# A two-layer diffusion trunk on one core: modulation weights in bursts, a narrow projection folded into a wide one, the convolution norm in more steps

## The chip, the cores and the metric

The kernel is one program on one core of a Trainium2 chip. The metric is the device time of that program in microseconds (us). All matrix work runs on TensorE (PE). VectorE is DVE, ScalarE is ACT, GpSimd is POOL; nearly all transfers are issued by SyncE (SP), whose queue is served in order. Each engine runs its own instructions strictly in the order of its queue, so an instruction that waits holds up all that stand behind it.

## The reference, cut to what matters

There are two token streams of 256 tokens, `x` and the context, with width 1024, and two layers. A layer modulates the normalized input by vectors computed from `c`, projects it, runs three branches (attention, gated linear attention or GLA, and a convolution module), merges them under gates, and ends with a feed-forward part.

```python
mod = (silu_c @ w_ada[l] + b_ada[l])[:, None, :]
sh1, sc1, g1, sh2, sc2, g2 = jnp.split(mod, 6, axis=-1)
proj = h @ p['w_in']
k, v, kg, vg, glr = _split(pm, MEM_SPLITS)        # glr: 32 columns, the low-rank gate input
k = _rmsnorm(_heads(k, N_KV_HEADS), p['k_norm'])
z = jnp.einsum('blnr,nrk->nblk', glr.reshape(B, L, 2, GLA_RANK), w_a2) + b_a[:, None, None, :]
o_gla = _rmsnorm(o_gla, p['gla_norm']).transpose(0, 2, 1, 3).reshape(B, L, GLA_V)
y = a * jax.nn.sigmoid(g)                          # then a depthwise convolution, 31 taps
y = jax.nn.silu(_layernorm(y, p['conv_ln_g'], p['conv_ln_b']))
return (g_att * y_att + g_gla * y_gla + g_conv * y_conv) @ p['w_out']
```

## The kernel before

Every large product is made of three matmuls in fp32r (`mm3`: high by high, high by low, low by high), because weights and activations are split into a high and a low part. A weight block of 128 x 1024 is loaded by SP into a `raw` buffer (5 of them), ACT copies it into `whi` (3 buffers), DVE subtracts into `wlo` (2 buffers); this is `wload`, lines 98 and 99. All large matmuls carry line 137. `fm` makes one feature-major product, 24 matmuls from one block. `tm` makes token-major products. Results lie in PSUM buffers of tag `mm` (4), `tr` (2) or `sd` (2).

Small work is written as Python generators (`attend`, `gla_head`, `conv_fin`, `ada_head`, `ada_gen`); `step` advances the first two in the list after each weight block, so their instructions fall between the large matmuls. Instructions are then put on the engines' queues by a planner with priorities, so the order of the queues is not that of the source.

`ada_head` computes the first two of a layer's modulation vectors: for each of four column groups j, four weight blocks of 512 KB (`ada`), eight fp32 matmuls at line 277 of 32 rows by 512 columns, each pair followed by a `yield`. The eight lie in four column groups of the array, `32 * (k % 4)`. In layer 0 it runs at the very start, with the loading and normalizing of the inputs (`run`, lines 815 to 834), and group j+1 is computed while the key and value projection (`kv`, with `start` called for each j) uses group j. In layer 1 it runs under the feed-forward part of layer 0. `ada_gen` does the rest of the vectors with four matmuls between yields (line 301).

`layer_consts` loads the taps, norms and rotation tables of a layer (`cols`, `qk`, `cs`). `gla_in` makes the inputs of a GLA head; `gla_prep` needs `glrT`, which is a whole `fm` product of its own from `wglr`, whose 128 columns are the 32 gate columns repeated. `gla_head` ends with a norm of each 128 x 256 output (`on`): ACT squares it with a sum (line 640), POOL makes the reciprocal root (93, 94), ACT copies it scaled (643), PE transposes it (649). `conv_fin` is the norm of the convolution: a matmul of ones over the sums (line 694) gives the means, DVE subtracts them from PSUM (702), ACT squares, POOL adds, a second product (714) gives the variance, DVE makes diagonal matrices (721), a third (725) spreads the reciprocal root, DVE multiplies from PSUM (731), ACT takes tanh and identity (737), and the result is split into `cvh` and `cvl` for the branch that multiplies by `w_conv_o`.

Of the kernel before, what the change touches and what calls it, by code (L numbers as in the profile page):

```python
# [52 lines left out]
class Trunk:  # L53
    BUFS = dict(hl=32, y=8, qt=8, kv=2, g=6, raw=5, whi=3, wlo=2, t4=4, tA=2, tB=4, pt=2, S=3, h1=6, sm=16, sa=16, sg=16, st=8,
                mc=4, cacc=1, jk=2, near=2)
# [198 lines left out]
    def ada_head(self, l, res):  # L254
# [8 lines left out]
        for j in range(4):  # L263
            ps = self.PS("sd")
            for i in range(4):
                if l == 0 and j % 2:
                    raw = [self.T("qt", [128, 512], name="ada") for _ in range(2)]
                    for kk in range(2):
                        nc.sync.dma_start(out=raw[kk], in_=I["w_ada0"][l, j, i][:, kk * 512:(kk + 1) * 512])
                else:  # L270
# [1 line left out]
                    nc.sync.dma_start(out=raw, in_=I["w_ada0"][l, j, i])
                    raw = [raw[:, :512], raw[:, 512:]]
                for kk in range(2):
                    k = 2 * i + kk
                    g = k % 4
                    nc.tensor.matmul(ps[32 * g:32 * g + 32, :], self.sc[:, k, :], raw[kk],  # L277
                                     start=(k < 4), stop=(k >= 4))
                yield
# [220 lines left out]
    def gla_head(self, h, kq, vg, og, last, me):  # L500
# [92 lines left out]
        for s in order:  # L593
# [35 lines left out]
            for c in range(2):  # L629
# [13 lines left out]
                nc.scalar.activation(out=on, in_=ps[:, :256], func=AF.Copy, scale=rs)  # L643
# [44 lines left out]
    def conv_fin(self, ys, ntok, hl):  # L688
# [5 lines left out]
        nc.tensor.matmul(pm[:, :ntok], self.onecol.to_broadcast([128, 128]), self.csum[:, :ntok], start=True, stop=True)
# [567 lines left out]
```

## Time and profile before

| | us |
|---|---|
| three runs | 1918.33, 1924.79, 1923.61 |
| median of them | 1923.61 |
| the profiled execution | 1923.12 |
| span of its instructions | 1921.1 |
| PE busy in the span | 1837.5 |
| DVE, ACT, POOL busy | 1300.9, 866.6, 167.5 |

The profiled execution lies 0.5 us under the median. Its time is 2.0 us more than the span. An idle time in brackets behind a row names what ended it. In rows of PE an fp32 matmul leaves two records, so "x4" on line 277 is two matmuls and "x8" on line 301 is four.

### The profile page before, as it was taken

The page shows a single profiled execution, that of the slowest core. Times are in us where ns is not written, and L with a number is a line of the kernel's source. Part 1 is how long each engine was busy: PE and PEld are TensorE (multiplying, and loading weights), DVE is VectorE, ACT ScalarE, POOL GpSimd, SP SyncE. Part 2 cuts the span into 40 slices and gives each one's busy share as a digit, 9 for nine tenths or more (in the row PEclk, how much of TensorE's full clock was granted, in tenths as well). Part 3 has the DMA queues.
Part 4 walks back from the last instruction along what each step waited for, and adds up shares of the span by engine and source line. Part 5 has one row for each costly group of instructions (what it writes and reads, how often), then busy time and mean ns, then how long its engine had stood idle before and what let it go on. Part 6 is the DMA issues. An engine that isn't in the chain of part 4 may idle for free.

```text
span 1921.1 us, 29251 instructions
## 1 busy us (share of the span) xinstructions
PE 1837.5 (96%) x11300; PEld 1498.2 (78%) x11300; DVE 1300.9 (68%) x2280; ACT 866.6 (45%) x1482; POOL 167.5 (9%) x235
## 2 busy tenths in 40 slices
PE   6999999999999999989999999989999999979998
PEld 2677788677777878867776888877888889969996
DVE  3597999987653445774333457689999777675656
ACT  2445434435733343453222334555455476445442
POOL 1111000012011001100000000031000200110000
PEclk8999999999999999989999999999999999989999
DMA  6421122632374334565466357643233435765663
GB/s 229 163 78 45 56 77 90 215 116 76 104 254 161 100 124 142 190 211 177 161 215 229 121 198 225 220 126 110 86 100 123 149 121 167 235 212 161 191 208 122
DMA packets 90892, 292.30 MB, mean 152 GB/s; under 512 B 10353, under 2 KB 12145, under 8 KB 90753
## 3 DMA queue, kind: packets, MB, share of 16 engines
q1 hardware_dynamic: 90752, 290.43, 46.8%
q8 instruction: 89, 1.46, 0.3%
q14 instruction: 51, 0.41, 0.1%
HBM read 277.77 MB, written 12.62 MB: 151 GB/s over the span
## 4 chain that ended last, share of the span: by engine, by line
PE 79%; DVE 10%; ACT 4%; issue 2%; POOL 2%; DMA 2%; SPq 0%; DVEq 0%; POOLq 0%; ACTq 0%
PE mm L137 66%; DVE acc L674 4%; DVE wlo L99 3%; PE sd L449 2%; PE sd L423 2%; PE sd L277 2%; PE mm L301 2%; PE sd L557 1%; PE sd L610 1%; ACT whi L98 1%; DMA ada<-in_w_ada 1%; PE sd L637 1%; PE tr L444 1%; POOL sg L94 1%; PE tr L344 1%
## 5 line engine op out<-in xcount | busy, mean ns | idle before, releaser
L99 DVE TENSOR_TENSOR wlo<-raw,whi 128x1024 fp32r<-128x1024 f32 x378 | 466.7, 1236 | 317.9 <-PE mm L137 230.9
L137 PE MATMUL mm<-hi,whi 128*128 128x512 f32 (+1 forms) x1920 | 657.5, 343 | 1.1 <-ACT whi L98 0.5
L137 PE MATMUL mm<-hi,wlo 128*128 128x512 f32 (+1 forms) x1920 | 650.5, 339 | 2.5 <-DVE wlo L99 2.3
L137 PE MATMUL mm<-lo,whi 128*128 128x512 f32 (+1 forms) x1920 | 651.4, 340 | 0.8 <-DVE lo L354 0.7
L98 ACT ACTIVATE whi<-raw 128x1024 fp32r<-128x1024 f32 x378 | 400.7, 1061 | 537.3 <-PE mm L137 416.8
L137 PEld LDWEIGHTS mm<-hi,whi 128*128 128x128 f32 x1920 | 364.5, 190 | 64.6 <-issue 12.7
L137 PEld LDWEIGHTS mm<-lo,whi 128*128 128x128 f32 x1920 | 365.2, 190 | 43.3 <-DVE lo L354 3.2
L137 PEld LDWEIGHTS mm<-hi,wlo 128*128 128x128 f32 x1920 | 364.5, 190 | 43.1 <-DVE wlo L99 4.8
L674 DVE SCALAR_TENSOR_TENSOR acc<-y,cols,acc 128x512 f32<-128x512 f32 (+1 forms) x464 | 288.5, 622 | 9.8 <-issue 0.2
L137 PE MATMUL mm<-wlo,hi 128*128 128x512 f32 (+1 forms) x676 | 238.6, 353 | 7.5 <-DVE wlo L99 7.5
L137 PE MATMUL mm<-whi,hi 128*128 128x512 f32 (+1 forms) x676 | 239.6, 356 | 0.6 <-ACT hi L352 0.6
L137 PE MATMUL mm<-whi,lo 128*128 128x512 f32 (+1 forms) x676 | 236.8, 351 | 0.0
L137 PEld LDWEIGHTS mm<-wlo,hi 128*128 128x128 f32 x676 | 127.6, 189 | 32.6 <-DVE wlo L99 9.9
L137 PEld LDWEIGHTS mm<-whi,hi 128*128 128x128 f32 x676 | 127.5, 189 | 22.1 <-issue 2.4
L137 PEld LDWEIGHTS mm<-whi,lo 128*128 128x128 f32 x676 | 127.5, 189 | 20.5 <-issue 2.5
L91 POOL TENSOR_SCALAR sm<-sm 128x1 f32<-128x1 f32 (+1 forms) x38 | 15.9, 418 | 756.9 <-DVE sm L332 664.6
L1036 POOL TENSOR_TENSOR mgp<-mgp,mgold 128x512 f32<-128x512 f32 x24 | 32.3, 1346 | 266.2 <-DVE mgp L1034 230.7
L277 PE MATMUL sd<-ada,sc 128*32 128x512 f32 x128 | 41.4, 703 | 11.8 <-DVE x L827 9.4
L449 PEld LDWEIGHTS sd<-pt,v 128*128 128x128 f32 x320 | 39.9, 191 | 16.0 <-ACT pt L446 12.1
L581 DVE TENSOR_TENSOR X<-X,sums 128x256 f32<-128x256 f32 (+1 forms) x112 | 47.6, 426 | 4.6 <-PE sd L557 3.3
L682 POOL TENSOR_TENSOR csum<-csum,y 128x512 f32<-128x512 f32 (+1 forms) x14 | 18.4, 1313 | 360.9 <-DVE y L674 360.9
L449 PE MATMUL sd<-pt,v 128*128 128x128 f32 x320 | 47.2, 286 | 2.6 <-ACT pt L446 1.1
(227 smaller groups left out, 2033.9 us busy)
## 6 DMA issues: line engine op xcount, KB each, us to landing
raw<-in_wfm SPq DMA_DIRECT2D x112, 512.0 KB
raw<-in_wff SPq DMA_DIRECT2D x94, 512.0 KB
raw<-in_wdown SPq DMA_DIRECT2D x66, 512.0 KB
raw<-in_w_ada SPq DMA_DIRECT2D x64, 512.0 KB
raw<-in_wbr SPq DMA_DIRECT2D x48, 512.0 KB
ada<-in_w_ada SPq DMA_DIRECT2D x24, 512.0 KB
raw<-in_wout SPq DMA_DIRECT2D x24, 512.0 KB
raw<-in_wq SPq DMA_DIRECT2D x16, 512.0 KB
```

The costliest lines, as they stand in the source:

```text
L94: nc.gpsimd.tensor_tensor(out=out, in0=t[:, :n], in1=self.mhalf.to_broadcast([128, n]), op=ALU.pow)
L98: nc.scalar.activation(out=hi, in_=src, func=AF.Copy)
L99: (eng or nc.vector).tensor_tensor(out=lo, in0=src, in1=hi.bitcast(F32), op=ALU.subtract)
L137: i = self.nc.tensor.matmul(*a, **k)
L277: nc.tensor.matmul(ps[32 * g:32 * g + 32, :], self.sc[:, k, :], raw[kk], start=(k < 4), stop=(k >= 4))
L301: nc.tensor.matmul(ps[32 * gg:32 * gg + 32, :], self.sc[:, k, :], raw[:, g * 512:(g + 1) * 512], start=(k == 0), stop=(k == KC - 1))
L344: nc.tensor.transpose(tr[:, kk, t * 128:(t + 1) * 128], xn[t][(k2 + kk) // 4][:, (k2 + kk) % 4 * 128:((k2 + kk) % 4 + 1) * 128], self.ident)
L423: nc.tensor.matmul(ps[:, :nk], qT[:, hh, :], self.kT[:, n, ko:512], start=True, stop=True)
L449: nc.tensor.matmul(po, self.v[:, ko // 128 + c, n * 128:(n + 1) * 128], pt[:, c, :], start=(c == 0), stop=(c == nkc - 1))
L581: nc.vector.tensor_tensor(out=a, in0=a, in1=t, op=ALU.mult)
L674: nc.vector.scalar_tensor_tensor(out=out, in0=win(y, sel, t), scalar=tap(t), in1=acc, op0=ALU.mult, op1=ALU.add)
L1036: nc.gpsimd.tensor_tensor(out=p, in0=p, in1=old, op=ALU.add)
```

## The change

- `ada_head`: in layer 0 all four blocks of a group are loaded and then all eight matmuls follow, the last block's first; in layer 1 two blocks at a time, four matmuls.
- `run` and `start`: all four input tiles are loaded ahead of the first modulation weights; they are normalized on ACT instead of DVE; `layer_consts(0)` comes after the third column group.
- `low_rank`: the 32 gate columns are appended to the value weights of GLA head 0 (`wvg0`, blocks of 128 x 1152, matmuls of 288 columns instead of 256); four copies on ACT repeat them, four transposes make `glrT`. The product from `wglr` is gone.
- `k_proc`: the scaling of the keys goes from DVE to POOL.
- `gla_head`: the output is copied out of PSUM unscaled and POOL scales it.
- `conv_fin`: three empty steps ahead of it, one ahead of each of the later products; means and reciprocal roots are copied by ACT into an SBUF buffer `cm`, from which DVE reads.

```diff
-                mc=4, cacc=1, jk=2, near=2)
+                mc=4, cacc=1, jk=2, near=2, cm=1)
-            raw = self.T("raw", [128, 1024])
+            raw = self.T("raw", [128, 1152])
...
-            for i in range(4):
...
-                for kk in range(2):
-                    k = 2 * i + kk
+            for n0 in (0,) if l == 0 else (0, 1):
+                parts = []
+                for i in range(4) if l == 0 else range(2 * n0, 2 * n0 + 2):
...
+                        parts += [(2 * i, raw[:, :512]), (2 * i + 1, raw[:, 512:])]
+                for n, (k, raw) in enumerate(parts[::-1]):
                     g = k % 4
-                    nc.tensor.matmul(ps[32 * g:32 * g + 32, :], self.sc[:, k, :], raw[kk],
-                                     start=(k < 4), stop=(k >= 4))
-                yield
+                    nc.tensor.matmul(ps[32 * g:32 * g + 32, :], self.sc[:, k, :], raw,
+                                     start=(n0 == 0 and n < 4), stop=(l > 0 and n0 == 1 or n >= 4))
+                if l:
+                    yield
...
-        nc.vector.tensor_tensor(out=kn, in0=kn, in1=rk.unsqueeze(2).to_broadcast([128, 2, 128]), op=ALU.mult)
+        nc.gpsimd.tensor_tensor(out=kn, in0=kn, in1=rk.unsqueeze(2).to_broadcast([128, 2, 128]), op=ALU.mult)
...
                 nc.scalar.activation(out=on, in_=ps[:, :256], func=AF.Square, accum_out=ss)
+                nc.scalar.activation(out=on, in_=ps[:, :256], func=AF.Copy)
                 rs = self.T("sg", [128, 1])
                 self.rstd(rs, ss, 1.0 / 256, EPS, 1, "sg")
-                nc.scalar.activation(out=on, in_=ps[:, :256], func=AF.Copy, scale=rs)
+                nc.gpsimd.tensor_tensor(out=on, in0=on, in1=rs.to_broadcast([128, 256]), op=ALU.mult)
...
+        for _ in range(3):
+            yield
         pm = self.PS("sd")
         nc.tensor.matmul(pm[:, :ntok], self.onecol.to_broadcast([128, 128]), self.csum[:, :ntok], start=True, stop=True)
+        cm = self.T("cm", [128, 512])
+        nc.scalar.activation(out=cm[:, :ntok], in_=pm[:, :ntok], func=AF.Copy)
...
+        yield
+        pv = self.PS("sd")
...
+        yield
         pr = self.PS("sd")
...
+        cm = self.T("cm", [128, 512])
+        nc.scalar.activation(out=cm[:, :ntok], in_=pr[:, :ntok], func=AF.Copy)
...
-        self.ada0 = self.ada_head(0, mod)
         for t in range(4):
-            if t == 2:
-                for _ in range(5):
-                    next(self.ada0)
...
-                nc.vector.tensor_scalar(out=x[n], in0=x[n], scalar1=mv[:, 0:1], scalar2=rs, op0=ALU.subtract,
-                                        op1=ALU.mult)
+                nc.scalar.activation(out=x[n], in_=x[n], func=AF.Identity, scale=rs, bias=nb)
             xn[t] = x
+        self.ada0 = self.ada_head(0, mod)
+        next(self.ada0)
         self.l = 0
-        self.layer_consts(0)
...
-            for _ in range(5):
-                next(self.ada0, None)
+            next(self.ada0, None)
+            if j == 2:
+                self.layer_consts(0)
...
-        pg = self.PS("mm")
-        self.fm(I["wglr"][l], pg, h)
...
+        def low_rank(g):
+
+            tr = self.PS("tr", (128, 4, 128))
+            for t in range(4):
+                nc.tensor.transpose(tr[:, t, :], g[:, t, :], self.ident)
...
+            n = 256 if hd else 288
+            ws = [self.wload(I["wvg"][l, hd, j] if hd else I["wvg0"][l, j], 4 * n, shift=112 if hd else 0) for j in range(2)]
```

The planner gives other queues. The first place is PE at the start, while column group 1 of layer 0's modulation (`ada`, into an `sd` buffer) is computed among the first matmuls of the key and value projection (`mm`, with `whi` and `wlo` its weights, `hi` and `lo` the modulated input). Before:

```order
L277 MATMUL sd_267<-ada_268,sc 32x512
L277 MATMUL sd_267<-ada_269,sc 32x512
L137 MATMUL mm_237<-whi_302,hi_202 128x512
L137 MATMUL mm_238<-whi_302,hi_202 128x512
L137 MATMUL mm_239<-whi_302,hi_202 128x512
L137 MATMUL mm_240<-whi_302,hi_202 128x512
L277 MATMUL sd_267<-ada_274,sc 32x512
L137 MATMUL mm_237<-wlo_303,hi_202 128x512
L137 MATMUL mm_237<-whi_302,lo_203 128x512
L137 MATMUL mm_237<-whi_302,hi_204 128x512
L277 MATMUL sd_267<-ada_275,sc 32x512
```

Now:

```order
L137 MATMUL mm_233<-whi_296,hi_196 128x512
L280 MATMUL sd_261<-ada_276,sc 32x512
L280 MATMUL sd_261<-ada_274,sc 32x512
L280 MATMUL sd_261<-ada_272,sc 32x512
L280 MATMUL sd_261<-ada_270,sc 32x512
L280 MATMUL sd_261<-ada_268,sc 32x512
L280 MATMUL sd_261<-ada_266,sc 32x512
L280 MATMUL sd_261<-ada_264,sc 32x512
L280 MATMUL sd_261<-ada_262,sc 32x512
L137 MATMUL mm_231<-whi_296,hi_198 128x512
L137 MATMUL mm_231<-wlo_297,hi_198 128x512
L137 MATMUL mm_231<-whi_296,lo_199 128x512
```

The eight matmuls that stood singly or in pairs among the projection's matmuls now stand in one run, and the first of them reads the block that is loaded last.

The second place is SP's queue at the same time. Before, behind the input tiles:

```order
L227 DMA cols_175<-in_cols 128x286
L234 DMA qk_180<-in_qknorm 128x256
L236 DMA cs_182<-in_cossin 128x512
L107 DMA raw_300<-in_wkv 128x1024
L269 DMA ada_268<-in_w_ada 128x512
L269 DMA ada_269<-in_w_ada 128x512
L269 DMA ada_274<-in_w_ada 128x512
L269 DMA ada_275<-in_w_ada 128x512
L269 DMA ada_280<-in_w_ada 128x512
L269 DMA ada_281<-in_w_ada 128x512
L269 DMA ada_286<-in_w_ada 128x512
L269 DMA ada_287<-in_w_ada 128x512
```

Now, behind the input tiles and the first column group:

```order
L276 DMA ada_165<-in_w_ada 128x1024
L107 DMA raw_294<-in_wkv 128x1024
L272 DMA ada_262<-in_w_ada 128x512
L272 DMA ada_264<-in_w_ada 128x512
L272 DMA ada_266<-in_w_ada 128x512
L272 DMA ada_268<-in_w_ada 128x512
L272 DMA ada_270<-in_w_ada 128x512
L272 DMA ada_272<-in_w_ada 128x512
L272 DMA ada_274<-in_w_ada 128x512
L272 DMA ada_276<-in_w_ada 128x512
L107 DMA raw_375<-in_wkv 128x1024
```

The three loads of `layer_consts(0)` (`cols`, `qk`, `cs`) are gone from this place; the first weight block and the second column group follow the first group at once.

The third place is ACT in layer 0, where GLA head 3's values are copied out of PSUM (`vg` from `mm`, ahead of the convolution's branch product). Before:

```order
L990 ACTIVATE kq_4623<-mm_4711 128x256
L98 ACTIVATE cvh_4822<-y_2560 128x512
L513 ACTIVATE X_4892<-kq_3785 128x2x256
L497 ACT_TABLE_LOAD
L497 ACTIVATE sums_4671<-sums_4671 128x1020
L497 ACTIVATE sums_4670<-sums_4670 128x1020
L98 ACTIVATE whi_5024<-raw_5022 128x1024
L1003 ACTIVATE vg_4624<-mm_4765 128x256
L1003 ACTIVATE vg_4624<-mm_4791 128x256
L1003 ACTIVATE vg_4625<-mm_4826 128x256
L1003 ACTIVATE vg_4625<-mm_4852 128x256
L539 ACTIVATE kk_4970<-X_4878 128x256
```

Now:

```order
L98 ACTIVATE cvh_4703<-y_774 128x512
L750 ACTIVATE y_1689<-y_1689,cols_464 128x2x256
L750 ACTIVATE th_4833<-y_2004,cols_464 128x512
L98 ACTIVATE cvh_4776<-y_1689 128x512
L98 ACTIVATE whi_5023<-raw_5021 128x1024
L750 ACTIVATE y_2004<-y_2004,cols_464 128x2x256
L750 ACTIVATE th_4842<-y_2271,cols_464 128x512
L750 ACTIVATE y_2271<-y_2271,cols_464 128x2x256
L98 ACTIVATE cvh_4837<-y_2004 128x512
L1024 ACTIVATE vg_4578<-mm_4719 128x256
L1024 ACTIVATE vg_4578<-mm_4745 128x256
L1024 ACTIVATE vg_4579<-mm_4780 128x256
```

Before, one of the norm's steps (`cvh`) stood within a dozen rows ahead of the copies; now eight of them (`th`, `y`, `cvh`) do, with a weight block among them.

More of the change, by code (lines that the diff above doesn't have):

```diff
@@ L116, in wload_hl @@
         with self.tc.high_priority(offset=self.ahead):
-            raw = self.T("raw", [128, 1024])
-            nc.sync.dma_start(out=raw, in_=src)
+            raw = self.T("raw", [128, 1152])
+            nc.sync.dma_start(out=raw[:, :1024], in_=src)
             his, los = [], []
@@ L295, in ada_gen @@
             for hf in range(2):
-                raw = self.T("raw", [128, 1024])
+                raw = self.T("raw", [128, 1152])
                 c0 = (r - 1) * 2048 + hf * 1024
-                nc.sync.dma_start(out=raw, in_=I["w_ada"][l, k * 128:(k + 1) * 128, c0:c0 + 1024])
+                nc.sync.dma_start(out=raw[:, :1024], in_=I["w_ada"][l, k * 128:(k + 1) * 128, c0:c0 + 1024])
                 for g in range(2):
@@ L699, in conv_fin @@
             yv = win(ys[g], slice(0, 2), 15)
-            mean = pm.rearrange("p (s t) -> p s t", t=256) if cpg == 1 else \
-                pm[:, :256].unsqueeze(1).to_broadcast([128, 2, 256])
+            mean = cm.rearrange("p (s t) -> p s t", t=256) if cpg == 1 else \
+                cm[:, :256].unsqueeze(1).to_broadcast([128, 2, 256])
             nc.vector.tensor_tensor(out=yv, in0=yv, in1=mean, op=ALU.subtract)
@@ L728, in conv_fin @@
             yv = win(ys[g], slice(0, 2), 15)
[L729 to L730 removed]
+            r = cm.rearrange("p (s t) -> p s t", t=256) if cpg == 1 else \
+                cm[:, :256].unsqueeze(1).to_broadcast([128, 2, 256])
             nc.vector.tensor_tensor(out=yv, in0=yv, in1=r, op=ALU.mult)
@@ L991, in gla_in @@
             step()
-            ws = [self.wload(I["wvg"][l, hd, j], shift=112) for j in range(2)]
+            n = 256 if hd else 288
+            ws = [self.wload(I["wvg"][l, hd, j] if hd else I["wvg0"][l, j], 4 * n, shift=112 if hd else 0) for j in range(2)]
+            if not hd:
+                low = self.T("tB", [128, 4, 128], name="low")
             for t in range(4):
-                ps = self.PS("mm", (128, 256))
+                ps = self.PS("mm", (128, n))
                 for k in range(KC):
                     hi, lo = ws[k // 4]
-                    s = slice(k % 4 * 256, (k % 4 + 1) * 256)
+                    s = slice(k % 4 * n, (k % 4 + 1) * n)
                     xh, xl = stat(t, k)
@@ L1002, in gla_in @@
                 with self.evac():
-                    nc.scalar.activation(out=vg[t // 2][:, t % 2, :], in_=ps, func=AF.Copy)
+                    nc.scalar.activation(out=vg[t // 2][:, t % 2, :], in_=ps[:, :256], func=AF.Copy)
+                    if not hd:
+                        nc.scalar.activation(
+                            out=low[:, t, :].rearrange("p (d r i) -> p d r i", d=2, r=4),
+                            in_=ps[:, 256:288].rearrange("p (d i) -> p d i", d=2).unsqueeze(2).to_broadcast(
+                                [128, 2, 4, 16]), func=AF.Copy)
                 if t % 2:
                     step()
+            if not hd:
+                low_rank(low)
             me = []
@@ L1227, in pack @@
     w2 = w2.reshape(L, 4, 128, 128)
-    glr = np.concatenate([2048 + 16 * d + np.arange(16) for d in (0, 0, 0, 0, 1, 1, 1, 1)])
+    vg0 = np.concatenate([w_in[:, :, 1024:1280], w_in[:, :, 2048:2080]], axis=2).reshape(L, 2, 4, 128, 288)
+    vg0 = vg0.transpose(0, 1, 3, 2, 4).reshape(L, 2, 128, 1152)
     cc = np.concatenate([np.broadcast_to(a.reshape(8, 128).T[:, :, None], (128, 8, 16)) for a in (c, c_ctx)], axis=2)
```

34 lines of the change are left out of this document (17 added, 17 removed).

## The prediction

> **What bounds the kernel now.** I read the page's busy times and the shares of the chain first, then what PE waited for, then the windows of the start.
>
> ```profile
> PE 1837.5 (96%) x11300; PEld 1498.2 (78%) x11300; DVE 1300.9 (68%) x2280; ACT 866.6 (45%) x1482; POOL 167.5 (9%) x235
> PE 79%; DVE 10%; ACT 4%; issue 2%; POOL 2%; DMA 2%; SPq 0%; DVEq 0%; POOLq 0%; ACTq 0%
> PE sd L277 <- DVE x L827: 9.4, 1, 9.4
> PE tr L649 <- ACT on L643: 6.5, 12, 1.2
> PE sd L694 <- POOL csum L682: 4.6, 2, 2.9
> PE sd L637 <- ACT on L643: 3.6, 4, 1.6
> PE sd L714 <- POOL csum L712: 1.3, 1, 1.3
> ```
>
> PE is busy 1837.5 of 1921.1 us and holds 79% of the chain, so a gain has to come from matrix work taken off PE, or from the start. The waits at the places that the change touches sum to 16 us beside the 9.4 us at the very start. The start, by windows, once for all engines (columns: window, PE, PEld, DVE, ACT, POOL, granted clock, DMA share, GB/s) and once for the modulation matmuls of line 277 alone (PE, PEld, clock, DMA):
>
> ```profile
> 0.00:9.30 9.30, 0.00 (x0) 0.00 (x0) 4.38 (x14) 1.70 (x2) 2.07 (x16) 1.00 0.75 241
> 9.30:25.60 16.30, 10.19 (x36) 2.98 (x36) 9.26 (x22) 3.64 (x7) 5.85 (x10) 0.79 1.04 407
> 25.60:40.90 15.30, 15.09 (x54) 7.09 (x52) 3.73 (x6) 2.71 (x6) 0.00 (x0) 0.89 0.15 48
> 25.60:40.90 15.30, 6.02 (x14) 0.74 (x12) 0.89 0.15 48
> 40.90:53.20 12.30, 4.25 (x19) 0.62 (x22) 1.00 0.79 273
> 53.20:66.50 13.30, 5.21 (x16) 0.66 (x16) 1.00 0.49 190
> 19.59 23.18 SPq L272 DMA_DIRECT2D ada<-in_w_ada  x4
> ```
>
> Up to 25.6 us the transfers are the limit (407 GB/s). From there PE is full, but only partly with the projection: of 40.9 us between 25.6 and 66.5, line 277 takes 6.02 + 4.25 + 5.21 = 15.5. The DMA share of 0.15 in the second stretch is SP standing for 23.18 us in the third group's loads, since `t4` buffers are taken.
>
> **Modulation in bursts.** The price of one insertion stands in layer 0's feed-forward part, where 24 matmuls alternate with one pair, and later with one group of four:
>
> ```profile
> 882.93 0.50 PE L137 MATMUL mm<-hi,whi 128*128 128x512 f32 x1
> 888.27 0.39 PE L137 MATMUL mm<-hi,wlo 128*128 128x512 f32 x1
> 888.59 1.05 PE L277 MATMUL sd<-ada,sc 128*32 128x512 f32 x4
> 889.57 0.50 PE L137 MATMUL mm<-hi,whi 128*128 128x512 f32 x1
> 946.42 0.39 PE L137 MATMUL mm<-hi,wlo 128*128 128x512 f32 x1
> 946.74 1.06 PE L301 MATMUL mm<-raw,sc 128*32 128x512 f32 x8
> 947.73 0.50 PE L137 MATMUL mm<-hi,whi 128*128 128x512 f32 x1
> 692.39 115.95 PE mm L137 x511
> ```
>
> A matmul of 512 columns takes 115.95 / 511 = 0.227 us, so 24 take 5.45; the period 882.93 to 889.57 is 6.64, so a pair costs 1.19. Four in four column groups cost the same: from the last matmul ahead of them to the first behind, 946.42 to 947.73 is 1.31, and 888.27 to 889.57 for the pair is 1.30. So the price goes by insertion, not by matmul.
>
> In layer 1's vectors PE's queue has 16 insertions before and 10 now; the six that go all lie behind the point where the feed-forward part runs without waits: 6 x 1.19 = 7.1 us. Ends: 3, if the held loads cost some of it back, and 9. I take -7.
>
> In layer 0 three groups fall among the projection, 15 insertions before, 3 runs of eight now. Eight are two rounds of four, 2 x 0.98 plus the change of form, some 2.1 us; three cost 6.3 instead of 15.5, a gain of 9.2 if the runs are warm. The first is not: the clock granted in these stretches is 0.79 and 0.89. On the other side, the first projection matmul starts at 25.6 now. The bytes ahead of it shrink by `cols`, `qk`, `cs` and the second group. Inputs and first group are 4.3 MB: 241 GB/s x 9.3 us are 2.2, the other 2.1 at 407 GB/s take 5.2, so they are in at 14.5 to 16 (the inputs' rows are half as long as the weights'). Eight matmuls at half the rate of the 0.98 per round take to 20, the copy, the small transposes and the modulation another 4 (an estimate). That is 24, a gain of 1.6, and about as much is lost again where the second run is cold too. I take -9 for the start. Ends: -3, if transfers keep setting the pace, and -13.
>
> `layer_consts(0)` comes later: `qk` now stands on SP behind the second block of the queries' weights. POOL's tables and keys wait for it, and so do PE's key transposes, which stand 84 matmuls x 0.227 = 19 us behind the projection in the queue. POOL needs some ten steps of 0.73 (row below) before the first of them, 8 us. So nothing, unless the load comes 10 us late; ends 0 and +5. The keys' scaling on POOL has the same cover. The inputs' normalization on ACT lies under the loading.
>
> **The low-rank product.** Per layer 24 matmuls of 512 columns go, 5.45 us. 96 matmuls grow by 32 columns. Nearest rows for 256 columns, and for transposes:
>
> ```profile
> 316.33 0.28 PE L137 MATMUL mm<-wlo,hi 128*128 128x256 f32 x1
> 316.45 0.28 PE L137 MATMUL mm<-whi,lo 128*128 128x256 f32 x1
> 65.41 1.03 PE L344 MATMUL tr<-ident,x 128*128 128x128 f32 x8
> ```
>
> 0.12 us per 256 columns is 0.015 per 32, 96 of them 1.4 us; four transposes of 1.03 / 8 = 0.13 and two changes of form are 0.8. So 5.45 - 2.2 = 3.2, twice 6.5 us less on PE. DVE and ACT lose one `wload` per layer and gain four small copies. New is a wait: `glrT` used to be ready long before its use; now 18 matmuls (4.1 us) cover ACT's copy and DVE's step, which stands behind two taps of 0.75. I charge +1 in all. Sum -5.5; ends -2 (wider matmuls at a worse rate) and -7.
>
> **Conv norm and GLA outputs.** The first product stands 38 matmuls later in layer 0 and 48 of half width in layer 1, over 5 us, against waits of 1.7 and 2.9: -4.6. The wait of 1.3 may stay, since POOL's chain of squares is the same; in layer 1 only 11 matmuls (1.3 us) now cover variance, root and diagonal, so +0.6. Together -4; ends -5.9 and 0.
>
> ```profile
> L643 ACT ACTIVATE on<-sd,sg 128x256 f32<-128x256 f32 x24 | 11.4, 473 | 19.9 <-POOL sg L94 19.9
> L387 POOL TENSOR_TENSOR kr<-kr,kn 128x256 f32<-128x256 f32 x4 | 2.9, 730 | 0.0
> ```
>
> The unscaled copy frees PSUM without POOL, so the 3.6 us at line 637 go. The chain to the transposes grows by 0.73 (POOL) less 0.47 (ACT), 0.3 with the queue 0.4; at some 8 of 24 places nothing covers it: +3.2. I take 0; ends -4 and +5.
>
> **A crowd that the queues show.** In layer 0 the second half of the conv norm now falls into the stretch in which GLA head 3's inputs are made. Between the third product of the norm and the copies of `vg`, ACT's queue holds 10 steps `th` and `y`, 4 `cvh`, 3 `whi`, 6 steps of `ea`, 2 of `sums`, 4 `kq`, 2 table loads and two small ones. Prices:
>
> ```profile
> 479.24 1.51 ACT L737 ACTIVATE y<-y,cols 128x512 f32<-128x512 f32 x2
> 498.41 1.27 ACT L481 ACTIVATE ea<-sd,cols 128x512 f32<-128x512 f32 x2
> 500.73 1.28 ACT L488 ACT_TABLE_LOAD   x1
> 503.09 1.05 ACT L98 ACTIVATE whi<-raw 128x1024 fp32r<-128x1024 f32 x1
> 504.04 0.63 ACT L990 ACTIVATE kq<-mm 128x256 f32<-128x256 f32 x2
> 504.56 0.63 ACT L98 ACTIVATE cvh<-y 128x512 fp32r<-128x512 f32 x1
> 507.83 2.00 ACT L497 ACTIVATE sums<-sums 128x1020 f32<-128x1020 f32 x2 [0.82 <-DVE sums L495]
> 516.40 1.21 ACT L1003 ACTIVATE vg<-mm 128x256 f32<-128x256 f32 x4 [2.14 <-PE sd L557]
> ```
>
> 10 x 0.73 + 4 x 0.55 + 3 x 1.0 + 6 x 0.6 + 2.0 + 1.3 + 2.6 + 0.8 = 22.8 us. PE needs 36 x 0.227 + 96 x 0.117 + 1.4 = 20.8 us for its share and then wants the next `mm` buffer, all four of which hold `vg` results. ACT also waits inside for DVE (sums, then the norm's products), which I put at 2.5 us. PE stands 22.8 + 0.3 + 2.5 - 20.8 = 4.8 us: I take +5. Before, ACT waited for PE there (2.14). Ends 0 and +12.
>
> **The sum.** -7 - 9 - 5.5 - 4 + 0 + 5 = -20.5 us on the profiled 1923.12: 1902.6, so 1902 to 1903 against a median of 1923.61.
>
> **The rivals.**
>
> *The start stays bound by transfers* (1910). For it: 1.04 of DMA share up to 25.6 us. Against: 0.15 right behind, and the bytes go down. Then the start gives 2 instead of 9.
>
> *The crowd costs more* (1914). ACT's queue also carries the feed of the next weights; if DVE's steps miss each other a second time, the stand is 15 to 17 instead of 5, and half of the gain is gone.
>
> *No crowd* (1896): ACT's steps overlap as well as in the rows above and PE never wants for `mm` buffers, and the GLA copies give their 3.6.
>
> *Slower: a run waits for its last load.* In layer 0's feed-forward part a run of four cannot start before both its blocks are in, and holds two of five `raw` buffers. If SP issues the second block only when the last run has freed a buffer, each of the 10 runs stands for the flight of a load:
>
> ```profile
> 833.53 5.55 DMA ada<-in_w_ada
>   issue: 10.7, 31
> ```
>
> (The second row is line 301's idle time, "issue", 10.7 us in 31 places.) At 5.5 us each that is 55, 1902 + 55 = 1957. It decides from 2.6 us per run (26 us over ten puts the time above 1929). Against it: line 301 already uses two `raw` blocks for a run, and none of its idle time is a wait for a load.
>
> *POOL holds DVE* (1910 to 1925). While POOL added for 1.5 us, a `wlo` that takes 1.24 in the mean took 2.1, 0.86 longer:
>
> ```profile
> 265.25 1.50 POOL L682 TENSOR_TENSOR csum<-csum,y 128x512 f32<-128x512 f32 x1 [36.65 <-DVE y L674]
> 265.74 2.10 DVE L99 TENSOR_TENSOR wlo<-raw,whi 128x1024 fp32r<-128x1024 f32 x1
> L99 DVE TENSOR_TENSOR wlo<-raw,whi 128x1024 fp32r<-128x1024 f32 x378 | 466.7, 1236 | 317.9 <-PE mm L137 230.9
> ```
>
> The 32 new POOL products of 0.73 are 23 us. By this row DVE loses 0.86 / 1.5 of that, 13, and at DVE's 10% of the chain PE loses 1.3; if every hold reached PE, 23, and the gain is gone at 1925. Against the full price: DVE idles 230.9 us for PE ahead of `wlo`. The Trainium skill speaks against the change here: "SBUF — State Buffer", section "Who interferes with whom", has a DVE instruction with two SBUF inputs and a POOL instruction that reads SBUF shut each other out entirely, whichever came first. By that rule it is the whole 23 us of DVE's time instead of 13, and 2.3 on PE instead of 1.3 by the same share. This row, 0.86 held of 1.5, agrees with a lock, as the rest of POOL's time lay ahead of the `wlo`.
>
> **How the numbers follow.** The forecast of 1902 has 0.58, the transfer-bound start 0.12, the larger crowd 0.10, no crowd 0.08, POOL's holds at their upper half 0.06, the waiting runs 0.06. Runs of this kernel span 0.3%, about what a measurement can tell from no change, or 5.8 us: faster means under 1918. The larger crowd is 0.02 within that, POOL's holds 0.05. So faster 0.87, same 0.07, slower 0.06. The range reaches from 1887, where the start gives 13, there is no crowd and the runs give 9, to 1916, where crowd and POOL each take their larger price.
>
> **What would show it.** In the changed trace: line 277's successor takes some 6 us between the first projection matmul and the end of the fourth group, and that group's projection ends near 63 instead of 72; DMA share is level there; matmuls of 288 columns stand 0.13 apart; no wait of PE for `csum` sums; fewer insertions but equal waits under the feed-forward part; and in layer 0, some 20 us after the norm's third product, PE waits about 5 us for ACT's `vg`. I am wrong if PE waits for `ada` at each run there, if the key transposes wait for POOL, or if DVE releases many more large matmuls than its 9.8 us.

## The result, and the profile after

The changed kernel takes 1895.53 us (median of 4 runs, 1894.05 to 1898.19) against 1924.2 for the kernel before on the same chip: ratio 0.9859, 95% interval 0.9835 to 0.9882. Its profiled execution has a span of 1892.3 us, 28.8 less than the 1921.1 of before. That is inside the range, and 6.5 us below the 1902 forecast.

Busy times, the engines' shares of the chain that ended last, and what PE waited for (total, times, longest):

```profile
PE 1803.7 (95%) x11260; PEld 1490.2 (79%) x11260; DVE 1301.5 (69%) x2266; ACT 869.6 (46%) x1498; POOL 189.9 (10%) x267
PE 74%; DVE 14%; ACT 5%; issue 3%; DMA 2%; POOL 2%; SPq 0%; POOLq 0%; DVEq 0%; ACTq 0%
PE sd L280 <- DMA ada<-in_w_ada: 16.7, 3, 15.7
PE tr L654 <- POOL on L648: 8.5, 8, 2.6
PE mm L137 <- DVE wlo L99: 6.8, 7, 3.2
PE sd L701 <- POOL csum L687: 3.9, 2, 2.9
```

PE is busy 33.8 us less. The forecast's terms for matrix work that goes sum to 22.8 (7.1, 9.2 and 6.5); the rest was not separated, and part of it stands beside a higher granted clock (rows below). PE's waits for the gated outputs on ACT at the state products (3.6) are gone, those at the transposes are 8.5 on POOL instead of 6.5 on ACT. The wait for the column sums, which I had taken to nothing, is 3.9 after 4.6. DVE's share of the chain rose from 10% to 14%. The start, for all engines and then for the modulation products of line 280 alone:

```profile
9.30:22.40 13.10, 5.67 (x32) 2.41 (x32) 4.98 (x17) 7.40 (x11) 2.35 (x6) 1.00 1.04 414
22.40:31.10 8.70, 8.69 (x48) 5.66 (x49) 3.69 (x7) 4.09 (x8) 0.00 (x0) 1.00 1.02 387
31.10:41.00 9.90, 9.68 (x57) 6.51 (x56) 3.60 (x7) 4.70 (x9) 0.00 (x0) 1.00 0.88 324
15.00:22.40 7.40, 3.64 (x16) 0.68 (x16) 1.00 1.04 410
41.00:50.00 9.00, 1.92 (x16) 0.42 (x16) 1.00 0.34 130
```

The granted clock is 1.00 and the DMA share level where the kernel before had 0.86, 0.62 and a hole (its rows stand with the load order below). The first run of eight takes 3.64 us, a later one 1.92.

To place gains I compare starts: the same product of PE in two traces, time in the kernel before minus time in the other. A gain that is made stays in all later rows of a column until something gives it back. The columns are eight of the thirteen traces other than that of before, each one execution.

| product (time before, us) | changed | mod. | low-rank | norms | mod. + low-rank | keys back | order | layer 1 runs |
|---|---|---|---|---|---|---|---|---|
| key transposes, layer 0 (86.4) | 14.1 | 9.9 | 0.3 | 1.2 | 7.5 | 6.8 | 7.3 | 0.5 |
| behind the low-rank product (320.0) | 17.2 | 9.3 | 4.4 | 0.7 | 11.5 | 10.8 | 7.2 | 0.5 |
| behind the conv norm, layer 0 (596.0) | 16.5 | 9.8 | 6.4 | 0.4 | 12.6 | 8.6 | 4.5 | 0.0 |
| behind layer 1's modulation (1209.6) | 25.8 | 17.3 | 10.3 | 2.1 | 22.1 | 19.0 | 6.8 | 7.8 |
| behind layer 1's low-rank product (1419.4) | 31.8 | 16.8 | 13.4 | 3.1 | 25.2 | 22.6 | 5.8 | 7.4 |
| first product of the last stage (1739.2) | 29.1 | 16.9 | 10.8 | 2.2 | 21.7 | 23.4 | 3.7 | 7.4 |

One execution is not the kernel, and at the start the difference is large. The seven traces with the new start have one order of PE's first 150 instructions, and still the small transposes of the fourth group start between 45.84 us ("modulation alone"; 46.04 in the changed kernel) and 49.08 ("keys back"). In the six with the old start they lie between 60.44 and 62.66, and the kernel before is the last of them. The changed kernel and "keys back" part behind the first run, where the same matmuls take 0.4 us in one and 0.63 in the other, with no wait and a granted clock of 1.00 in both; here one such matmul and the second run of each:

```profile
22.98 0.40 PE L137 MATMUL mm<-whi,hi 128*128 128x512 f32 x1
24.23 1.92 PE L280 MATMUL sd<-ada,sc 128*32 128x512 f32 x16
24.74 0.63 PE L137 MATMUL mm<-whi,hi 128*128 128x512 f32 x1
27.00 2.22 PE L280 MATMUL sd<-ada,sc 128*32 128x512 f32 x16
```

At the key transposes the four traces with the changed start and the keys on POOL gained 14.1, 13.2, 11.6 and 11.4 against the one trace of before. Against all six old starts that is 9 to 14, and 11.7 between the means. So the 14.1 is the upper end, and differences of up to 3 us between columns of the first row may be the execution's.

### The profile page after: what moved, and what is told of

Its sections match the earlier page's. It is cut to its first block, busy times and chain, and to the rows that moved or that the text cites. A ratio compares the mean times of both kernels' runs of the same rounds, so it can differ in the third digit from the quotient of the medians.

```text
span 1892.3 us, 29210 instructions
## 1 busy us (share of the span) xinstructions
PE 1803.7 (95%) x11260; PEld 1490.2 (79%) x11260; DVE 1301.5 (69%) x2266; ACT 869.6 (46%) x1498; POOL 189.9 (10%) x267
## 4 chain that ended last, share of the span: by engine, by line
PE 74%; DVE 14%; ACT 5%; issue 3%; DMA 2%; POOL 2%; SPq 0%; POOLq 0%; DVEq 0%; ACTq 0%
PE mm L137 62%; DVE acc L679 5%; DVE wlo L99 4%; PE sd L453 2%; PE sd L427 2%; PE mm L305 1%; PE sd L614 1%; PE sd L641 1%; PE sd L561 1%; ACT whi L98 1%; PE sd L280 1%; PE tr L448 1%; DMA ada<-in_w_ada 1%; DMA raw<-in_wff 1%; DVE u L784 0%
## 5 line engine op out<-in xcount | busy, mean ns | idle before, releaser
L99 DVE TENSOR_TENSOR wlo<-raw,whi 128x1024 fp32r<-128x1024 f32 (+1 forms) x376 | 469.8, 1251 | 312.5 <-PE mm L137 221.8
L137 PE MATMUL mm<-hi,whi 128*128 128x512 f32 (+1 forms) x1904 | 649.8, 342 | 1.6 <-ACT whi L98 0.8
L137 PE MATMUL mm<-lo,whi 128*128 128x512 f32 (+1 forms) x1904 | 643.3, 338 | 3.1 <-DVE lo L358 2.9
L98 ACT ACTIVATE whi<-raw 128x1024 fp32r<-128x1024 f32 (+1 forms) x376 | 399.3, 1063 | 534.8 <-PE mm L137 384.2
L137 PE MATMUL mm<-hi,wlo 128*128 128x512 f32 (+1 forms) x1904 | 643.6, 338 | 0.5 <-DVE wlo L99 0.5
L137 PEld LDWEIGHTS mm<-hi,whi 128*128 128x128 f32 x1904 | 359.8, 189 | 59.7 <-issue 14.3
L137 PE MATMUL mm<-wlo,hi 128*128 128x512 f32 (+2 forms) x676 | 239.6, 354 | 6.3 <-DVE wlo L99 6.3
L137 PE MATMUL mm<-whi,hi 128*128 128x512 f32 (+2 forms) x676 | 240.9, 357 | 1.3 <-ACT hi L356 1.3
L137 PE MATMUL mm<-whi,lo 128*128 128x512 f32 (+2 forms) x676 | 237.7, 353 | 0.0
L137 PEld LDWEIGHTS mm<-wlo,hi 128*128 128x128 f32 x676 | 127.8, 189 | 25.8 <-DVE wlo L99 8.4
L137 PEld LDWEIGHTS mm<-whi,lo 128*128 128x128 f32 x676 | 127.8, 189 | 17.3 <-DVE lo L358 1.2
L687 POOL TENSOR_TENSOR csum<-csum,y 128x512 f32<-128x512 f32 (+1 forms) x14 | 16.8, 1201 | 395.4 <-DVE y L679 395.4
L453 PEld LDWEIGHTS sd<-pt,v 128*128 128x128 f32 x320 | 39.9, 191 | 15.7 <-ACT pt L450 11.6
L543 ACT ACTIVATE kk<-X 128x256 f32<-128x256 f32 x72 | 29.8, 419 | 37.8 <-DVE X L592 37.5
```

The lines of the kernel that those rows point to most:

```text
L98: nc.scalar.activation(out=hi, in_=src, func=AF.Copy)
L99: (eng or nc.vector).tensor_tensor(out=lo, in0=src, in1=hi.bitcast(F32), op=ALU.subtract)
L137: i = self.nc.tensor.matmul(*a, **k)
L453: nc.tensor.matmul(po, self.v[:, ko // 128 + c, n * 128:(n + 1) * 128], pt[:, c, :], start=(c == 0), stop=(c == nkc - 1))
L543: nc.scalar.activation(out=cap(out[s], 0, [[2 * lev, nb], [lev, 2], [1, lev]]), in_=cap(X[s], W, [[2 * lev, nb], [2 * W + lev, 2], [1, lev ...
```

## The experiments

Theory M: each part brings its own gain, where the starts show it. Rivals: the gain of the start is the runs, or the load order; the norms pay, or cost. All ratios are to the kernel before.

**Modulation alone** (the first block's loads behind the x tiles, runs of eight and of four, constants late, x normalized on ACT):

```diff
-        self.ada0 = self.ada_head(0, mod)
         for t in range(4):
-            if t == 2:
-                for _ in range(5):
-                    next(self.ada0)
...
+        self.ada0 = self.ada_head(0, mod)
+        next(self.ada0)
         self.l = 0
-        self.layer_consts(0)
...
+            next(self.ada0, None)
+            if j == 2:
+                self.layer_consts(0)
```

> The kernel before with the modulation's part of the change alone: the loads and products of layer 0's first modulation block after the four x tiles, eight products in a run, layer 1's in runs of four, x normalized on ScalarE. By the milestones of the two traces (the same product of TensorE, before minus after) the start gave 14.1 us and the stretch with layer 1's feed-forward blocks 8.6, so theory M (each part brings its own gain) expects 22 to 23 us less, about 1901. Rival R (part of the start's 14 comes from the other edits, through loads that move) expects 10 to 17 us less, about 1910. The prediction's own terms for these edits were 9 and 7, so 16.

1911.98 us, ratio 0.9941 (0.9925 to 0.9956): 11 less, in the range of rival R, half of what theory M expects. The profiled execution, at 1906.45 the shortest of six, has 16.9 by the table: 16.8 at the fourth group's modulation, of which only 9.9 are left at the key transposes.

**Low-rank product alone** (32 columns more in head 0's weight block, no product of its own):

```diff
-        self.fm(I["wglr"][l], pg, h)
...
+                nc.tensor.transpose(tr[:, t, :], g[:, t, :], self.ident)
...
+            n = 256 if hd else 288
```

> The kernel before with the low-rank product folded into head 0's value and gate columns, and nothing else. Theory M, by the milestones: 4.7 us in layer 0 and 4.6 in layer 1, so 9 less, about 1915. The prediction's term was 5.5, about 1918.5. Rival T (the transposes and copies that the fold adds are paid on the path when no norm has moved): 0 to 3 less, about 1922.

1912.59 us, 0.9946 (0.9934 to 0.9958): 10.4 less, twice the prediction's term. PE's rows at the end of the product in the kernel before, then with the fold:

```profile
301.59 0.50 PE L137 MATMUL mm<-hi,wlo 128*128 128x512 f32 x1 [1.24 <-DVE wlo L99]
306.80 0.50 PE L479 MATMUL sd<-glrT,w 64*128 64x512 f32 x2
L137 PE MATMUL mm<-wlo,hi 128*128 128x288 f32 x32 | 9.5, 298 | 1.1 <-DVE wlo L99 1.1
295.69 0.49 PE L969 MATMUL tr<-ident,low 128*128 128x128 f32 x3
301.81 0.50 PE L479 MATMUL sd<-glrT,w 64*128 64x512 f32 x2
```

The product that needs the result starts 5.0 us earlier (0.3 of it was there from the start). DVE is full there (busy 4.89 of the 5 us from 300 us on in the kernel before), and with the product went a wait of 1.24 for its own weights' low halves; the wait for those of head 0's values stays (1.1). The first product at line 479 waits for nothing. The transposes cost PE some 0.4 us, by the starts of the matmuls around them (295.56 to 295.94 and 297.18 to 297.53). Rival T is out.

**Norms alone** (keys, gated outputs, conv norm):

```diff
-        nc.vector.tensor_tensor(out=kn, in0=kn, in1=rk...
+        nc.gpsimd.tensor_tensor(out=kn, in0=kn, in1=rk...
...
+                nc.scalar.activation(out=on, in_=ps[:, :256], func=AF.Copy)
...
+                nc.gpsimd.tensor_tensor(out=on, in0=on, in1=rs...
...
+        for _ in range(3):
+            yield
...
+        nc.scalar.activation(out=cm[:, :ntok], in_=pm[:, :ntok], func=AF.Copy)
```

> The kernel before with the norms alone: keys scaled on GpSimd, gated outputs copied unscaled and scaled on GpSimd, the conv norm over more steps with its mean and rstd in SBUF. The prediction's terms were 4 off for the conv norm, 0 for the gated outputs and 5 on for the crowd on ScalarE: about 1 slower, 1925. Theory M, by the milestones (4.4 lost in layer 0 where ScalarE is full, 2.7 lost in layer 1): 5 to 7 slower, about 1930. Rival N (the crowd comes only from the low-rank copies that stand beside it, so without them the shorter waits show): 4 to 8 faster, about 1918.

1917.61 us (12 runs, 1915.53 to 1925.16), 0.9975 (0.9963 to 0.9986): 4.8 less, so theory M, read off the starts of the changed kernel, was wrong in sign. The time lies in the range of rival N, whose reason (the low-rank copies as the crowd) it does not show. The profiled execution was the slowest of the twelve, and is taken up below.

**Modulation and low-rank together**, the norms as before:

> The changed kernel with the norms and the keys as before: modulation and low-rank edits together. Theory M: the gains add, 22.7 + 9.3 = 32 less than before, about 1892, so 3 to 4 below the changed kernel's 1895.5. By the prediction's terms it would lose nothing by the crowd but miss the conv norm's 4: 16 + 5.5 = 21.5 less, about 1902, a little above the changed kernel. Rival N (the norms bring a gain that the milestones hide): 5 us or more above the changed kernel, about 1901.

1901.98 us, 0.9890 (0.9875 to 0.9904). The two gains add (11.3 + 10.4 against 21.2), and the norms are worth another 6.5 on top (6.0 by the ratios). The next three runs ask where.

**Keys back on DVE** in the changed kernel:

```diff
-        nc.gpsimd.tensor_tensor(out=kn, in0=kn, in1=rk...
+        nc.vector.tensor_tensor(out=kn, in0=kn, in1=rk...
```

> The changed kernel with the keys scaled on VectorE again, as before. In the runs with the modulation edit alone and with modulation and low-rank edits, VectorE's queue stands in these four multiplies for GpSimd's rotary chain, and the weights' low halves behind them reach TensorE 3.6 and 3.1 us late (rows at 73.03 and 75.18), with a granted clock of 0.83 behind it. Theory H (VectorE's queue stands for GpSimd because the constants come later): that wait of 3 to 4 us is back and the time is 4 to 6 above the changed kernel, about 1900.5. The prediction's own reading (the edit costs and brings nothing, for it has the projection's cover): 1895.5. Rival G (the whole gain of the norms, 6.5, lies in the GLA outputs and the conv norm): 1895.5 too, and no wait for the low halves at 70 us.

1900.55 us, 0.9883 (0.9861 to 0.9904): 5.0 above the changed kernel (4.6 by the ratios), as theory H said. Rows of POOL, DVE and PE with the keys back, then the changed kernel's, then two of "conv norm back" (below), which has the keys on POOL too:

```profile
59.52 3.80 POOL L241 TENSOR_TENSOR rope<-cs,qk 128x256 f32<-128x256 f32 x4 [45.44 <-DMA qk<-in_qknorm]
68.58 0.43 DVE L377 TENSOR_TENSOR kr<-kr,sm 128x256 f32<-128x256 f32 x1 [4.39 <-POOL kr L391]
73.84 0.43 DVE L377 TENSOR_TENSOR kn<-kn,sm 128x256 f32<-128x256 f32 x1 [0.86 <-POOL sm L94]
74.44 2.35 DVE L99 TENSOR_TENSOR wlo<-raw,whi 128x1024 fp32r<-128x1024 f32 x2
75.72 0.80 PE L137 MATMUL mm<-hi,wlo 128*128 128x512 f32 x1 [3.01 <-DVE wlo L99]
...
56.51 3.81 POOL L241 TENSOR_TENSOR rope<-cs,qk 128x256 f32<-128x256 f32 x4 [42.65 <-DMA qk<-in_qknorm]
67.98 3.35 DVE L99 TENSOR_TENSOR wlo<-raw,whi 128x1024 fp32r<-128x1024 f32 x2
69.83 0.50 PE L137 MATMUL mm<-hi,wlo 128*128 128x512 f32 x1 [0.17 <-DVE wlo L99]
...
59.23 3.80 POOL L241 TENSOR_TENSOR rope<-cs,qk 128x256 f32<-128x256 f32 x4 [45.55 <-DMA qk<-in_qknorm]
70.68 3.36 DVE L99 TENSOR_TENSOR wlo<-raw,whi 128x1024 fp32r<-128x1024 f32 x2
```

The constants come late, so POOL's rotary chain starts at 56.5 to 59.5 us; with the keys back DVE's queue then stands four times for POOL (two of them shown). The `wlo` behind comes 6.5 us later than in the changed kernel, but 3.0 of that is the late start of this execution, which the chain on POOL has as well. Against "conv norm back", whose chain starts 0.3 earlier, the `wlo` comes 3.8 later: 3.5 is the queue's. PE waits 3.01 for it, and the granted clock from 70 to 80 us is 0.83 (1.00 in the two others). On POOL the scaling stands behind the steps that it needs, and DVE's queue is free.

**Gated outputs back** (scaled in ACT's copy) and **conv norm back**, each in the changed kernel:

```diff
-                nc.scalar.activation(out=on, in_=ps[:, :256], func=AF.Copy)
...
-                nc.gpsimd.tensor_tensor(out=on, in0=on, in1=rs...
+                nc.scalar.activation(out=on, in_=ps[:, :256], func=AF.Copy, scale=rs)
```

The second undoes all lines of `conv_fin` in the change.

> The changed kernel with the gated outputs scaled in ScalarE's copy again. The prediction's term was 0: the 3.6 us at line 637's successor come back, and 3.2 go at the transposes: 1895.5. By the waits of the runs without the norms (3.0 at the products, 5.9 at the transposes, against 8.5 now) it is 0.4 slower, 1896. Rival G (the unscaled copy frees PSUM earlier and gains more than that): 3 us or more slower, 1899.

1894.55 us, 0.9847 (0.9826 to 0.9868).

> The changed kernel with the conv norm as before, in two stretches and read from PSUM. The prediction's terms: the waits of 4 come back and the crowd of 5 on ScalarE in layer 0 goes, so 1 faster, 1894.5. Theory M, by the milestones (2 to 4 us lost in layer 0 between the norm's third product and the modulation products behind it, and the wait for the column sums still 3.9): 2 to 4 faster, 1892. Rival G (the spread norm is what brings the 6.5): 4 to 6 slower, about 1900.

1896.14 us, 0.9856 (0.9833 to 0.9878). Neither moves the time by what can be told. PE's waits around layer 0's and layer 1's conv norm in the changed kernel, then with the old norm:

```profile
PE sd L701 <- POOL csum L687: 1.0, 1, 1.0
PE mm L137 <- ACT vg L1024: 0.5, 1, 0.5
PE sd L701 <- POOL csum L687: 2.9, 1, 2.9
...
PE sd L699 <- POOL csum L687: 0.9, 1, 0.9
PE sd L699 <- POOL csum L687: 2.6, 1, 2.6
```

The same waits for the same sums; and PE's wait for ACT's `vg`, the crowd of the prediction, is 0.5.

**Load order alone** in the kernel before (the edit of the first experiment, constants late and x normalized on ACT, with the products left in pairs in both layers):

```diff
+        self.ada0 = self.ada_head(0, mod)
+        for _ in range(5):
+            next(self.ada0)
         self.l = 0
-        self.layer_consts(0)
...
+            if j == 2:
+                self.layer_consts(0)
```

> The kernel before with the order of the start alone: the modulation's first loads behind the x tiles, the layer's constants behind the third block of queries, x normalized on ScalarE; the products stay in pairs, 15 insertions among the projection, and layer 1 as before. The prediction put all but 1.6 of the start's gain of 9 on the insertions. Theory I (insertions): no hole of 23 us on SyncE's queue, but the pairs cost as before, and VectorE's queue stands for the keys as in the run with the modulation edit alone: 0 to 4 less than before, about 1921.5. Rival L (the load order with its level transfers and warm clock is the start's gain, and the runs of eight bring little): 7 to 10 less, about 1915.

1917.57 us (12 runs, 1914.04 to 1924.25), 0.9974 (0.9959 to 0.9988): 5.0 less, between theory I and rival L. Start of each group's small transposes, the last step of its modulation: before (first and fourth group), order alone, modulation alone; and the windows of before and of order alone:

```profile
15.77 1.05 PE L284 MATMUL tr<-sel,m 128*128 128x2 f32 x8 [0.79 <-DVE m L281]
62.66 0.95 PE L284 MATMUL tr<-sel,m 128*128 128x2 f32 x8
17.05 1.05 PE L284 MATMUL tr<-sel,m 128*128 128x2 f32 x8 [0.79 <-DVE m L281]
53.95 0.95 PE L284 MATMUL tr<-sel,m 128*128 128x2 f32 x8
20.05 1.05 PE L288 MATMUL tr<-sel,m 128*128 128x2 f32 x8 [0.83 <-DVE m L285]
45.84 0.96 PE L288 MATMUL tr<-sel,m 128*128 128x2 f32 x8
9.30:22.40 13.10, 7.54 (x29) 2.28 (x29) 6.86 (x19) 1.93 (x4) 3.03 (x7) 0.86 1.05 404
22.40:31.10 8.70, 8.15 (x18) 2.66 (x18) 4.12 (x6) 3.82 (x6) 2.82 (x4) 0.62 0.64 237
31.10:41.00 9.90, 9.68 (x43) 5.21 (x42) 2.00 (x3) 0.70 (x2) 0.00 (x0) 1.00 0.01 2
9.30:22.40 13.10, 9.46 (x41) 3.15 (x41) 5.28 (x18) 9.51 (x16) 2.35 (x6) 1.00 1.04 413
22.40:31.10 8.70, 8.70 (x31) 3.67 (x31) 1.54 (x3) 1.88 (x4) 0.00 (x0) 1.00 1.03 414
```

At the fourth group the order is worth 8.7 us (62.66 to 53.95; 6.5 from the earliest of the old starts) and the runs another 8.1 (to 45.84; 4.9 to the latest of the new ones). At the first group the run costs 3.0 (17.05 to 20.05), since it waits for all its loads. With the order alone PE is full and at clock 1.00 from 22.4 us on, where before had 0.62: both theories had a half. What the normalization on ACT does in it was not separated. The constants came earlier here than in the changed kernel: `qk` is issued at 37.05 us instead of 52.49, POOL's chain starts at 42.43, and PE has no wait for `wlo` behind the keys.

**Keys alone** on POOL, in the kernel before:

> The kernel before with one line changed: the keys scaled on GpSimd. Putting them back on VectorE cost the changed kernel 5.0 us. Theory H (that price exists only where the constants come late, for there VectorE's queue stands for GpSimd's rotary chain; before, the chain was over in time): 0 to 1.5 less, about 1923, and none of the 6.2 of the three norm edits alone. Rival K (VectorE's queue stands for GpSimd in the kernel before too): 4 to 6 less, about 1918.

1926.53 us (12 runs), 1.0009 (0.9993 to 1.0024): nothing, theory H again. Where the constants come first, the edit takes away no wait.

**Layer 1's runs alone**:

```diff
+            if l == 0:
+                for i in range(4):
...
+            else:
+                for n0 in (0,) if l == 0 else (0, 1):
...
+                    if l:
+                        yield
```

> The kernel before with layer 1's modulation products in runs of four instead of pairs, and nothing else. The prediction's term was 7 (6 rounds of 1.19); the milestones of the run with the modulation edit alone give 7.5, those of the changed kernel 8.6: 7 to 9 less, about 1915.5. Rival W (runs of four stand for the loads of their second block): 0 to 3 less, about 1922, with waits for the load at these products.

1916.41 us, 0.9960 (0.9946 to 0.9974): 7.7 less. The 64 products of layer 1, before and with runs (shortest, median and longest in ns, first and last start):

```profile
L277 PE MATMUL sd<-ada,sc x64: 592/617/1062, 820.2 to 928.7; 128*32 128x512 f32 x64
L297 PE MATMUL sd<-ada,sc x64: 592/617/1062, 820.2 to 880.1; 128*32 128x512 f32 x64
PE sd L277 <- DMA ada<-in_w_ada: 2.4, 1, 2.4
PE sd L297 <- DMA ada<-in_w_ada: 0.7, 1, 0.7
```

The same products, four side by side as fast as two, done 48.6 us earlier, and with less waiting for loads, not more.

**Only what paid** (gated outputs and conv norm as before, the rest changed):

> The changed kernel with the gated outputs and the conv norm as before: modulation, low-rank fold and keys on GpSimd. Theory H (of the norms only the keys pay): the run without any of them took 1902.0, the keys are worth 5 to 6: 1896, as fast as the changed kernel. By the two single reversals (1.0 less and 0.6 more): 1895. Rival (outputs and norm need each other, for the spread norm fills what the unscaled copy frees): 1899 or more.

1898.38 us (4 runs), 0.9872 (0.9857 to 0.9887): no better than the changed kernel, whose interval it overlaps. Its trace reaches the last stage at 1709.3 us, 0.8 ahead of the changed kernel's 1710.1, and loses 4.3 there, by what the last run shows. Whether the other three executions did so isn't known, so theory H and its rival (1899 or more) stay undecided by 1898.4.

**Norms alone, profiled again**:

> The three norm edits alone, a second execution under the profiler: the first took 1925.2 where half of its runs took under 1917.7. In the first, the 256-column products of the last stage (from 1740 us on) start 117.8 ns apart and in the kernel before 113.3, at the same granted clock, which is 4.9 us over the stage. Theory P (a stage runs at one of two paces from its start, and the runs of a kernel differ by which stages took which): at about 1916 the last stage is at 113.3, and the rest of the difference lies in other whole stages whose spacing is 113 to 114 instead of 117 to 118. Rival Q (the difference is waits, of TensorE for transfers or for other engines): the same spacings, fewer or shorter waits.

1919.42 us, one run. The same 30 us of the last stage in the first profile and in the second:

```profile
1775.00:1805.00 30.00, 30.00 (x257) 30.00 (x256) 18.45 (x19) 14.86 (x17) 0.00 (x0) 1.00 0.63 188
1775.00:1805.00 30.00, 30.00 (x267) 30.00 (x266) 18.54 (x19) 14.71 (x17) 0.00 (x0) 1.00 0.65 194
```

257 or 267 products, PE full and the clock at 1.00 in each. The trace of "only what paid" has 257 there too, the kernel before 267. Over the 960 products of that stage all 14 traces have one of two lengths, 108.80 us (113.33 ns a product) or 113.07 (117.78), and the two executions of this kernel one each. Theory P holds for the last stage; the two starts of it differ by only 1.3 us (1737.0 and 1735.7), with nearly the same waits.

## Why the prediction was right or wrong

- **Layer 1's runs, -7**: right (7.7 alone, 7.8 by the starts). That they would wait for their loads is out: 0.7 us.
- **Start, -9**: 14.1 by the starts of the two profiles, 9 to 14 over all traces with either start. The term for the runs was near or too large (9.2 by the working, 4.9 to 8.1 measured). The step that failed is the load order, which I charged at 1.6 and cancelled against a cold second run: it is 6.5 to 8.7 at the fourth group, and the second run took 1.92 to 2.22 us and not the first one's 3.64. In the two profiles some 2.5 of the gain at the fourth group (16.6) are gone again at the key transposes; what takes them was not separated. A row of the kernel before that the sum left out goes with the order, PE's waits for x tiles whose loads stood behind the first group's; they are gone with the order alone, and so is the granted clock of 0.62 beside them:

```profile
PE tr L344 <- DVE x L827: 5.2, 2, 3.0
```

- **Constants late and keys on POOL, 0**: I priced each by its own cover. They are one edit: behind the runs of eight, late constants without the keys on POOL cost what "keys back" shows, about 5, and the keys' scaling alone brings nothing. My cover of 19 us was counted for PE and POOL; what was late stood in DVE's queue, in front of the weights.
- **Low-rank product, -5.5**: 10.4 alone. The term that was too small is layer 0's, 4.7 to 5.0 instead of 2.75: a wait of 1.24 went with the product, the transposes cost less than the 0.8 charged, and the new wait that I charged did not come. In layer 1 the gain is 3.1 behind the product with the fold alone (6.0 in the changed kernel), and 4 are given back at the column sum: its first product starts 9.3 us earlier than before, where the products ahead of it were 13.6 earlier. DVE alternates taps and `wlo` without a gap up to that point (to 1491.6 us in the changed kernel), so PE only waits there. Another 4 come up between 835 and 857 us, beside a higher granted clock (before, then with the fold, whose trace is 6.4 us ahead here):

```profile
820.00:840.00 20.00, 14.99 (x84) 9.91 (x82) 16.60 (x36) 11.64 (x21) 3.67 (x8) 0.78 0.59 207
840.00:860.00 20.00, 19.49 (x126) 16.36 (x122) 12.41 (x21) 10.69 (x18) 0.93 (x2) 0.79 0.63 196
820.00:840.00 20.00, 17.27 (x116) 13.61 (x115) 16.97 (x35) 11.04 (x20) 2.88 (x6) 0.91 0.61 199
840.00:860.00 20.00, 19.57 (x144) 15.38 (x143) 10.39 (x22) 13.49 (x26) 0.85 (x2) 1.00 0.65 222
```

  From 20 to 40 us behind layer 1's first modulation product the granted clock is 0.94 to 1.00 in all seven traces with the fold, 0.77 to 0.91 in six without it and 1.00 in the seventh (order alone). So it mostly goes with the fold; why stays open.

- **Conv norm, -4, and the crowd, +5**: both too large, and by luck the mistakes cancelled; the whole edit is worth 0.6 in one direction or the other. The wait for the sums stayed at 3.9, since in layer 1 (2.9 of it) the sums are set by DVE's taps, not by where the product stands; POOL's last addition in the changed kernel shows it, behind 24.00 us of waiting for DVE. The crowd's 4.8 us was a wait of 0.5.

```profile
1490.58 1.48 POOL L687 TENSOR_TENSOR csum<-csum,y 128x256 f32<-128x256 f32 x1 [24.00 <-DVE y L679]
```

- **Gated outputs, 0**: right, 1.0 and within the measurement. The 3.6 us at the state products went, and the transposes wait 2.0 longer instead of 3.2.
- **POOL holds DVE**: the split of the weights slowed from 1236 (the row in the prediction) to 1251 ns, 5.6 us over 376 of them, against 13 to 23 in that rival:

```profile
L99 DVE TENSOR_TENSOR wlo<-raw,whi 128x1024 fp32r<-128x1024 f32 (+1 forms) x376 | 469.8, 1251 | 312.5 <-PE mm L137 221.8 <-issue 56.3 <-ACT whi L98 31.4
```

  By the Trainium skill's rule ("SBUF — State Buffer", "Who interferes with whom") the rival had the full 23; this kernel shows about a quarter of it on this group, and other DVE steps were not separated.

By stretches of the table the changed kernel gained 14.1 at the start (forecast 9), 3.1 at layer 0's low-rank product (2.75), lost 0.7 to the end of layer 0's conv norm (forecast: 1.7 gained, 5 lost), gained 9.3 to the end of layer 1's modulation (7) and 3.3 behind it (2.75 and 2.3). That is 8.6 more than the terms, against 8.3 by the spans and 6.5 from 1902 to the median: 5 of it the start with the keys (of which 2.4 lies in this pair of executions), 2.6 the crowd that did not come, 2.3 at layer 1's modulation, where the clock is part of it, less 1.8 that DVE kept.

The time came out at the rival "no crowd" (1896, chance 0.08), and its condition held, but the crowd is only 2.6 of these 8.6 us: most of the miss was in the start, which that rival left as it was. The range's lower end is not the sum of the three ends that it names: they come to 1891.6, and 1887 takes the gated outputs' 4 as well. The result lies above both.

Open: alone, the norms gained 4.8 by the ratio with the keys worth nothing, while the two profiles show 2.2 and 3.5 at the last stage's first product and the single reversals nothing; the pace of whole stages, 4.3 us in one of them, is as large as what is left.

## What to carry to other kernels

Price a moved load by the queue of every engine that touches its data, not by the engine that you protect: here it was DVE, a third party, that stood with the weights behind it, and moving four small multiplies from its queue to that of the engine that they waited for was worth about 5 us, but only together with the move. Before spreading a step to hide a wait, ask which engine sets its input: a product that is issued later waits as long if a full DVE makes its operand. And where a stage can take two paces, compare starts ahead of that stage, and not spans, for effects of a few us, and take several executions, for here starts of one order differed by 3 us.

## What was not expected of the hardware

- The last stage's products of 256 columns run at 113.33 or 117.78 ns each from the stage's first to its 960th, at granted clock 1.00 and with PE full; the same kernel shows both. Nothing in the rows says what picks one. The Trainium skill ("TensorE: Matmul & The Clock Gate", section "Back-to-back issue gap") gives N / 2.4 + 2.5 ns as the warm gap of an isolated product, by estimate 109.2 ns for 256 columns, and says that in a stream of weight loads and matmuls both set the spacing. Both paces here lie above that estimate, by 4 and by 9 ns.
- The first run of eight took 3.64 us and the later ones 1.92, though the granted clock reads 1.00 for each. How long the slower pace lasts differs between executions: behind the first run the matmuls took 0.4 us from 22.8 us on in the changed kernel, and 0.63 up to 27 us with the keys back.
- Interrupted PE at the start stood beside a granted clock of 0.62 (22.4 to 31.1 us before); the same stretch without the waits had 1.00.
